# Regrouping the gate/up block products of a hybrid encoder layer: four weight sums a side, three chained pairs, plain token order

## The chip, the cores and the metric

The kernel runs on one core of a Trainium2 chip. A core has a matmul engine (PE, with its weight loads shown apart as PEld), a vector engine (DVE), a scalar engine (ACT), a third elementwise engine (POOL) and SP, whose queue issues most DMAs. Each works off its own instruction queue in order, and they meet at semaphores. Elementwise operands lie in on-chip memory (SBUF); matmul results lie in banks of PSUM, which ACT and DVE read out ("evacuate"). The metric is device microseconds of one launch, the median of several runs.

## The reference, cut to what matters

```python
def encoder_layer(x, ...):
    h = rmsnorm(x, attn_norm_g)
    proj = h @ w_in
    ...
    mix = jnp.concatenate([rmsnorm(a, mla_out_g), rmsnorm(b, na_out_g)], axis=-1)
    x = x + mix @ w_o
    h2 = rmsnorm(x, ffn_norm_g)
    x = x + (jax.nn.silu(h2 @ w_gate) * (h2 @ w_up)) @ w_down
    return x
```

Two sequences (256 and 1024 tokens, model width 1024, FFN width 2816) go through the layer in float32 and then through a last norm. The change touches `h2 @ w_gate` and `h2 @ w_up`, and what prepares `h2`.

## The kernel before, in words

The 1280 tokens are ten tiles of 128. Every float32 operand of a matmul is split into two fp32r parts, hi (a cast, on ACT) and lo (the rest, a subtraction on DVE or POOL), and `mm3` (L108) issues three matmuls: hi by hi, hi by lo, lo by hi.

**Stages.** Projections and attention come first. The output projection follows (691 to 830 us of the profile): for each token tile t, `mix_in` prepares the mixed heads, `out_proj` runs 48 matmuls of 512 columns into `po` and adds the residual (L786), and `ffn_in` (L788) makes the normalised `h2` (Square on ACT L792, its root on POOL L89/L91, the scaling on DVE L795), transposes it into two PSUM banks of 4 x 128 columns (L818) and reads those out, times a gain, into the four activation blocks R11, R12, R21, R22 (first digit: upper or lower half of the model width; second: tokens 0 to 639 or 640 to 1279; held in tiles zA and zB). Then gate and up run together, and then the down projection (matmuls into `d`).

**Gate and up.** The product of a weight panel (2 x 2 blocks A of 512 x 128) and the activations (2 x 2 blocks R) is made with seven block products instead of eight (Strassen's way). There are 11 panels `fp` and two sides (gate i=0, up i=1). Product m multiplies a weight operand `wc` (a block or a sum of blocks, split into hi and lo) by an activation operand `S[m]` (a block or a sum of blocks, split likewise): 4 slices kc x 3 matmuls x 2 halves s of 320 columns, so 24 matmuls into two banks `M`. In all 11 x 2 x 7 x 24 = 3696 matmuls.

`operand` (L862) makes a weight operand: the sum on POOL (L870, five of the seven products have one), the cast on ACT (L873), the lo on POOL (L874); three operands fit in `wc`. `S[1]` and `S[3]` are built tile by tile in the output projection; the others (6, 5, 2, 4, 7) in the first panel, by `build_S`: a sum on DVE or POOL (L838), a cast on ACT (L843) and a lo on DVE (L844). `product` reads a finished bank once or twice: a copy on ACT (L931), or an add or subtraction on DVE (L934, L936). `finish` makes the silu (ACT L949), gate times up (DVE L951), and the sums and stores of the activations for the down projection (L964, L70).

**Order.** Token tiles go 0, 5, 1, 6, 2, 7, 3, 8, 9, 4, so that the sums of R blocks of two token halves can be made early. Products go 3, 6, 1, 5, 2, 4, 7; in the first panel 3 and 1 first, mixed over sides and halves. The order on PE, ACT, DVE and POOL is fixed when the program is built, by a scheduler that keeps program order only where it is told (`tc.issue_after`); on the chip each engine follows its list.

Of the kernel before, what the change touches and what calls it, by code (L numbers as in the profile page):

```python
# [11 lines left out]
F32 = mybir.dt.float32  # L12
# [27 lines left out]
def encoder_trunk(ctx: ExitStack, tc: tile.TileContext, x_tm, x_T, g_attn, w_c, w_v, w_qk,  # L40
# [67 lines left out]
    def mm3(out, sh, sl, mh, ml, first, last):  # L108
        nc.tensor.matmul(out, lhsT=sh, rhs=mh, start=first, stop=False)  # L109
        nc.tensor.matmul(out, lhsT=sh, rhs=ml, start=False, stop=False)  # L110
        nc.tensor.matmul(out, lhsT=sl, rhs=mh, start=False, stop=last)  # L111
# [605 lines left out]
    for x in reversed(lstack):  # L717
# [14 lines left out]
         3: [rC.tile([P, 4, NQ], F32R, name="S3", bufs=2) for x in "hl"]}  # L732
# [55 lines left out]
    def ffn_in(t, x, sum1=None):  # L788
# [9 lines left out]

        def evacuate(eng, q, tr, add=None):
            for i in range(4):  # L800
                s = gf[:, 4 * q + i:4 * q + i + 1]
                o = R[f"{q + 1}{t // 5 + 1}"][:, i, c0:c0 + P]
                if add is not None:
                    eng.scalar_tensor_tensor(out=sum1[:, i], in0=tr[:, i], scalar=s,
                                             in1=add[:, i, c0:c0 + P], op0=ALU.mult, op1=ALU.add)
                elif eng is nc.scalar:
                    eng.activation(o, tr[:, i], AF.Copy, scale=s)
                else:
                    eng.tensor_scalar(out=o, in0=tr[:, i], scalar1=s, scalar2=1.0,
                                      op0=ALU.mult, op1=ALU.mult)  # L810

        tr = []
        for q in range(2):
            tr.append(po.tile([P, 4, P], F32, name="trm" if t in order[-2:] and q else "trh",
                              bufs=1))
            for i in range(4):
                kc = 4 * q + i
                nc.tensor.transpose(tr[q][:, i], h2[:, kc * P:(kc + 1) * P], ident)  # L818
            if sum1 is None:
                evacuate(nc.vector if q else nc.scalar, q, tr[q])  # L820
            elif q == 0:
                evacuate(nc.vector, 0, tr[0], R["22"])
        if sum1 is not None:
            out = split_S(1, slice(c0, c0 + P), sum1)
            with tc.issue_after(out[0]):
                evacuate(nc.scalar, 0, tr[0])
            evacuate(nc.vector, 1, tr[1])
            return out


    B_OP = {1: ("11", ALU.add, "22"), 3: ("12", ALU.subtract, "22"), 6: ("11", ALU.add, "12"),
            5: ("22",), 2: ("11",), 4: ("21", ALU.subtract, "11"), 7: ("21", ALU.add, "22")}

    SUM = {6: R["12"], 4: R["11"], 7: R["21"], 5: R["22"], 2: R["11"]}

    def sum_S(m, cs, eng, out=None):
        a, op, b = B_OP[m]
        return eng.tensor_tensor(out=SUM[m][:, :, cs] if out is None else out,  # L838
                                 in0=R[a][:, :, cs], in1=R[b][:, :, cs], op=op).ins

    def split_S(m, cs, src=None):
        src = SUM[m][:, :, cs] if src is None else src
        i0 = nc.scalar.copy(out=S[m][0][:, :, cs], in_=src)  # L843
        i1 = nc.vector.tensor_sub(out=S[m][1][:, :, cs], in0=src, in1=S[m][0][:, :, cs])  # L844
        return i0.ins, i1.ins

    def make_S(m, cs, eng):
        tmp = rY.tile([P, 4, P], F32, name="sum", bufs=2)
        sum_S(m, cs, eng, tmp)
        return split_S(m, cs, tmp)  # L850

    A_OP = {1: ("11", ALU.add, "22"), 3: ("11",), 6: ("21", ALU.subtract, "11"),
            5: ("11", ALU.add, "12"), 2: ("21", ALU.add, "22"), 4: ("22",),
            7: ("12", ALU.subtract, "22")}

    def load_A(src, fp, blocks, at=None):
        A = {}
        for b in blocks:
            nm = at[b] if at else b
            A[b] = rY.tile([P, 4, P], F32, name=f"A{nm}", bufs=2 if nm == "11" else 1)  # L860
            load(A[b], src[fp, int(b[0]) - 1, int(b[1]) - 1])
        return A  # L862

    def operand(A, m):
        if len(A_OP[m]) == 1:
            raw = A[A_OP[m][0]]
        else:
            a, op, b = A_OP[m]
            raw = rY.tile([P, 4, P], F32, name="sum", bufs=2)
            nc.gpsimd.tensor_tensor(out=raw, in0=A[a], in1=A[b], op=op)  # L870
# [5 lines left out]

    src = (w_gate, w_up)

    def first(m, i):
        at = {"11": "11", "12": "21", "21": "12", "22": "11"} if i else None  # L880
        return operand(load_A(src[i], 0, [b for b in A_OP[m] if isinstance(b, str)], at), m)

    pm = [pool("pm0", space=PSUM, side="right")]
    order = (0, 5, 1, 6, 2, 7, 3, 8, 9, 4)
    cur = mix_in(order[0])
    w31 = {}
    for n, t in enumerate(order):
        with tc.issue_after(last_split[0]):
            nxt = mix_in(order[n + 1]) if n + 1 < NT else None
        if n == 6:  # L890
            w31 = {(m, i): first(m, i) for m, i in ((3, 0), (3, 1), (1, 0))}
        out_proj(t, *cur)
        cs = slice((t % 5) * P, (t % 5 + 1) * P)
# [372 lines left out]
```

## Time and profile before

| | us |
|---|---|
| median of 3 runs | 1672.1 (1670.27 to 1674.97) |
| the profiled execution, its own time | 1669.73 |
| its span, first to last instruction | 1667.8 |
| PE busy (PEld, DVE, ACT, POOL) | 1607.0 (1450.4, 950.5, 751.4, 689.2) |

```profile
PE   7999999999899999999989999999999998999998
DVE  4653044445677777544486555444555546855776
ACT  5534154444577777544354333333333333333434
POOL 3451434353011119234387666767666650000102
```

The four rows are from the page's picture of the span in 40 slices of 41.7 us, a digit being the busy share in tenths. The output projection lies in slices 17 to 20, gate and up in 20 to 33, the down projection behind. PE is close to full in nearly all; the eight in slice 21 is the passage from the output projection to gate and up, that in slice 34 the passage to the down projection. POOL is busiest in gate and up, where it makes the weight sums and the lo parts, and still has three to four tenths free.

### The profile page before, as it was taken

How to read it: one execution, taken by the hardware profiler on the slowest of the kernel's cores; microseconds unless marked ns; L12 is line 12 of the kernel's file. 1: busy time of each engine (PE TensorE's matmuls, PEld its weight loads, DVE VectorE, ACT ScalarE, POOL GpSimd, SP SyncE). 2: the span in 40 equal slices, each digit the busy share in tenths (PEclk: the TensorE clock that was granted, in tenths of full speed). 3: DMA queues.
4: the chain of work that ended last, by engine and by line, in shares of the span. 5: the costliest groups of instructions: out<-in, count | busy, mean ns of one | idle time of the engine just before them, and what ended most of it. 6: DMA issues, size and time to landing. Idle time of an engine off the chain costs nothing.

```text
span 1667.8 us, 26037 instructions
## 1 busy us (share of the span) xinstructions
PE 1607.0 (96%) x9601; PEld 1450.4 (87%) x9601; DVE 950.5 (57%) x1641; ACT 751.4 (45%) x1565; POOL 689.2 (41%) x818
## 2 busy tenths in 40 slices
PE   7999999999899999999989999999999998999998
PEld 7987899987688888888879999999999997788886
DVE  4653044445677777544486555444555546855776
ACT  5534154444577777544354333333333333333434
POOL 3451434353011119234387666767666650000102
PEclk9999999999999999999999999999999999999999
DMA  6635302134001013234332322222322219733434
GB/s 225 207 108 141 67 23 61 36 114 145 20 19 34 20 29 99 76 122 144 115 108 94 107 93 86 76 90 83 107 106 81 77 64 358 245 93 95 147 104 150
DMA packets 125231, 173.75 MB, mean 104 GB/s; under 512 B 35568, under 2 KB 67184, under 8 KB 125104
## 3 DMA queue, kind: packets, MB, share of 16 engines
q1 hardware_dynamic: 80864, 122.92, 23.3%
q10 hardware_dynamic: 43680, 46.87, 8.2%
q0 software_dynamic: 560, 2.29, 0.3%
q8 instruction: 76, 1.25, 0.3%
q14 instruction: 51, 0.42, 0.1%
HBM read 121.58 MB, written 50.46 MB: 103 GB/s over the span
## 4 chain that ended last, share of the span: by engine, by line
PE 84%; issue 4%; DMA 4%; POOL 3%; ACT 2%; DVE 2%; SPq 0%; POOLq 0%; ACTq 0%; DVEq 0%
PE M L111 10%; PE M L110 10%; PE M L109 10%; PE d L110 5%; PE d L109 5%; PE d L111 5%; PE o L685 3%; PE tp L678 3%; PE na_o L461 2%; PE po L109 2%; PE pj L109 2%; PE pj L111 2%; PE pj L110 2%; PE po L110 2%; PE po L111 2%
## 5 line engine op out<-in xcount | busy, mean ns | idle before, releaser
L109 PE MATMUL M<-S,wc 128*128 128x320 f32 x1056 | 326.8, 310 | 2.8 <-ACT wc L873 2.3
L110 PE MATMUL M<-S,wc 128*128 128x320 f32 x1056 | 327.4, 310 | 2.1 <-DVE S L844 2.0
L111 PE MATMUL M<-S,wc 128*128 128x320 f32 x1056 | 325.3, 310 | 1.4 <-POOL wc L874 1.4
L109 PEld LDWEIGHTS M<-S,wc 128*128 128x128 f32 x1056 | 198.9, 188 | 3.8 <-ACT wc L873 2.8
L110 PEld LDWEIGHTS M<-S,wc 128*128 128x128 f32 x1056 | 198.8, 188 | 3.2 <-DVE S L844 3.1
L874 POOL TENSOR_TENSOR wc<-sum,wc 128x512 fp32r<-128x512 f32 x110 | 148.7, 1353 | 128.0 <-ACT wc L873 125.7
L111 PEld LDWEIGHTS M<-S,wc 128*128 128x128 f32 x1056 | 198.2, 188 | 1.9 <-POOL wc L874 1.9
L870 POOL TENSOR_TENSOR sum<-A,A 128x512 f32<-128x512 f32 x110 | 162.3, 1483 | 13.6 <-DMA A<-in_w_gate_dram 4.2
L873 ACT CAST wc<-sum 128x512 fp32r<-128x512 f32 x110 | 68.0, 622 | 188.2 <-PE M L110 142.8
L110 PE MATMUL d<-w,ah 128*128 128x512 f32 x385 | 147.4, 398 | 2.5 <-DVE w L1029 2.5
L109 PE MATMUL d<-w,ah 128*128 128x512 f32 x385 | 144.5, 400 | 4.2 <-ACT ah L1028 4.2
L111 PE MATMUL d<-w,ah 128*128 128x512 f32 x385 | 145.4, 398 | 0.4 <-DVE ah L1029 0.4
L934 DVE TENSOR_TENSOR z<-M,z 128x320 f32<-128x320 f32 x144 | 67.8, 485 | 88.0 <-PE M L111 51.1
L100 DVE TENSOR_TENSOR PT<-tp,PT 128x512 fp32r<-128x512 f32 (+1 forms) x144 | 93.1, 658 | 40.6 <-ACT PT L99 39.2
L1028 ACT CAST ah<-as 128x640 fp32r<-128x640 f32 x77 | 56.0, 727 | 121.7 <-issue 71.3
L934 DVE TENSOR_TENSOR zB<-M,zB 128x320 f32<-128x320 f32 x120 | 56.6, 486 | 81.2 <-PE M L111 47.6
L99 ACT CAST PT<-tp 128x512 fp32r<-128x512 f32 (+1 forms) x144 | 79.1, 564 | 42.4 <-PE tp L678 39.3
L109 PEld LDWEIGHTS d<-w,ah 128*128 128x128 f32 x385 | 73.1, 190 | 22.8 <-ACT ah L1028 5.0
L1029 DVE TENSOR_TENSOR ah<-as,ah 128x640 fp32r<-128x640 f32 x77 | 64.1, 836 | 50.4 <-ACT ah L1028 50.4
L670 DVE TENSOR_REDUCE mm<-S 128x1 f32<-128x1024 f32 (+1 forms) x80 | 84.8, 1061 | 12.7 <-PE S L111 11.2
L698 POOL TENSOR_TENSOR ob<-ob 128x128 f32<-128x128 f32 x40 | 18.4, 461 | 177.5 <-ACT ob L695 177.3
L110 PEld LDWEIGHTS d<-w,ah 128*128 128x128 f32 x385 | 72.7, 189 | 20.7 <-DVE w L1029 3.2
(384 smaller groups left out, 4004.8 us busy)
## 6 DMA issues: line engine op xcount, KB each, us to landing
as<-act_d SPq DMA_DIRECT2D x77, 320.0 KB
A<-in_w_gate_dram SPq DMA_DIRECT2D x52, 256.0 KB
A<-in_w_up_dram SPq DMA_DIRECT2D x52, 256.0 KB
act_d<-z ACTq DMA_DIRECT2D x35, 320.0 KB
act_d<-zB ACTq DMA_DIRECT2D x35, 320.0 KB
x<-in_x_tm_dram SPq DMA_DIRECT2D x20, 512.0 KB
cT_d<-stg ACTq DMA_DIRECT2D x20, 320.0 KB
w<-in_w_down_dram SPq DMA_DIRECT2D x11, 512.0 KB
```

The costliest lines, as they stand in the source:

```text
L99: i = nc.scalar.copy(out=hi, in_=ps)
L100: nc.vector.tensor_sub(out=lo, in0=ps, in1=hi)
L109: nc.tensor.matmul(out, lhsT=sh, rhs=mh, start=first, stop=False)
L110: nc.tensor.matmul(out, lhsT=sh, rhs=ml, start=False, stop=False)
L111: nc.tensor.matmul(out, lhsT=sl, rhs=mh, start=False, stop=last)
L670: nc.vector.reduce_max(out=nm[:, u:u + 1], in_=S, axis=AX.X, negate=True)
L870: nc.gpsimd.tensor_tensor(out=raw, in0=A[a], in1=A[b], op=op)
L873: i0 = nc.scalar.copy(out=hi, in_=raw)
L874: i1 = nc.gpsimd.tensor_tensor(out=lo, in0=raw, in1=hi, op=ALU.subtract)
L934: nc.vector.tensor_add(out=o, in0=ps, in1=o)
L1028: nc.scalar.copy(out=o[:, 0], in_=raw)
L1029: nc.vector.tensor_sub(out=o[:, 1], in0=raw, in1=o[:, 0])
```

## The change

The seven products are grouped in another way (still seven, still 3696 matmuls). With s1 = A21 + A22, s2 = s1 - A11, s4 = A12 - s2 and A21' = A11 - A21 a side needs four sums; products 1 and 2 take plain blocks A11 and A12. On the activation side R11 and R21 are used plainly by products 1 and 2, and for tokens 640 to 1279 the blocks are combined as they leave PSUM. Second members of the pairs 1-2, 7-4 and 5-3 go on accumulating in the PSUM bank of the first (`CHAIN`, `held`, `onto`), after that bank has been read once; so a bank is read once for each of the seven products. The order of products is 1, 2, 6, 7, 4, 5, 3, that of tokens 0 to 9.

For tokens 0 to 639, `ffn_in` splits R11 and R21 straight into S1 and S2. For tokens 640 to 1279 both banks of a tile are read twice, slice by slice: ACT writes the plain block, and DVE (`scalar_tensor_tensor`) writes R12 - R11 or R22 - R21 over the old block. Then come a further sum T2 into a tile of its own and R21 - T2 (POOL; DVE for the last tile). S6 is cast from T2 by token tiles.

In the first panel four products (1 and 2, of gate and of up) come first, the operands of three of them made at token tile 6; the six other weight blocks of the panel are loaded, once the output projection has ended, into memory that will later hold S5 (`spare`), and the sums of both sides are made there before product 6.

```diff
-    A_OP = {1: ("11", ALU.add, "22"), 3: ("11",), 6: ("21", ALU.subtract, "11"),
-            5: ("11", ALU.add, "12"), 2: ("21", ALU.add, "22"), 4: ("22",),
-            7: ("12", ALU.subtract, "22")}
...
+            for i in range(4):
+                s = gf[:, 4 * q + i:4 * q + i + 1]
+                o = R[f"{q + 1}{t // 5 + 1}"][:, i, cs]
+                if t < 5 and q:
+                    nc.vector.tensor_scalar(out=o, in0=tr[q][:, i], scalar1=s, scalar2=1.0,
+                                            op0=ALU.mult, op1=ALU.mult)
+                else:
+                    nc.scalar.activation(o, tr[q][:, i], AF.Copy, scale=s)
+                if t >= 5:
+
+                    d = R["12" if q else "11"][:, i, cs]
+                    nc.vector.scalar_tensor_tensor(out=d, in0=tr[q][:, i], scalar=s, in1=d,
+                                                   op0=ALU.mult, op1=ALU.subtract)
+        if t < 5:
+            split_S(1, cs)
+            split_S(2, cs)
+            return
+        eng = nc.vector if t == NT - 1 else nc.gpsimd
...
+        eng.tensor_tensor(out=T2[t - 5], in0=R["22"][:, :, cs], in1=R["11"][:, :, cs],
+                          op=ALU.subtract)
+        return eng.tensor_tensor(out=R["21"][:, :, cs], in0=R["21"][:, :, cs], in1=T2[t - 5],
+                                 op=ALU.subtract).ins
...
+    def operand(A, m, s2=None, s4=None):
+        if m == 6:
...
+            sum_A(A["s1"], A["21"], A["22"], ALU.add)
+            sum_A(A["s2"], A["s1"], A["11"])
+            w = split_A(A["s2"])
...
+            sum_A(A["s4"], A["12"], A["s2"])
+            return w
+        if m == 7:
+            sum_A(A["21"], A["11"], A["21"])
+        return split_A(A[{1: "11", 2: "12", 7: "21", 4: "22", 5: "s1", 3: "s4"}[m]])
...
-    order = (0, 5, 1, 6, 2, 7, 3, 8, 9, 4)
...
-    SEQ2 = (3, 6, 1, 5, 2, 4, 7)
+    SEQ = (1, 2, 6, 7, 4, 5, 3)
+    CHAIN = {2: 1, 4: 7, 3: 5}
...
+        if m not in CHAIN:
+            held[s] = pm[bank].tile([P, 512], F32, name=f"M{bank}", bufs=4)[:, 0:NS]
+        ps = held[s]
...
             mm3(ps, w[0][:, kc], w[1][:, kc], S[m][0][:, kc, cs], S[m][1][:, kc, cs],
-                kc == 0, kc == 3)
...
+                kc == 0 and m not in CHAIN, kc == 3, m in CHAIN)
...
+            for n, (b, i) in enumerate((("12", 1), ("21", 0), ("22", 0), ("21", 1), ("22", 1),
+                                        ("12", 0))):
+                A0[i][b] = load_A(i, 0, b, at[n])
+            for i in range(2):
+                for m in (1, 2):
+                    for s in range(2):
+                        product(C[i], w0[m, i], m, s, held[i], 0)
+                    finish(G, U, i, m, fp)
+                if i == 0:
+                    w0[2, 1] = operand(A0[1], 2)
+            for n, m in enumerate(SEQ[2:]):
+                w = [operand(A0[i], m, at[6 + i], ("A21", "A22")[i]) for i in range(2)]
+                if m != 3:
+                    build_S(SEQ[n + 3], w[1][2:])
```

Three places show what the scheduler made of it. The first is ACT's list at the last token tile. Before, `zA<-trh` of x4 reads one whole bank (half of the last tile), `M0` and `M1` are product banks, and `wc` operands:

```order
L843 CAST S1_7998<-sum_9192 128x4x128
L807 ACTIVATE zA_8002<-trh_9201,gf_8022 128x128 x4
L843 CAST S6_9243<-zA_8003 128x4x320
L931 COPY z_9250<-M0_9341 128x320
L843 CAST S6_9243<-zA_8003 128x4x320
L931 COPY z_9249<-M1_9326 128x320
L873 CAST wc_9377<-sum_9375 128x512
L931 COPY z_9250<-M1_9356 128x320
L873 CAST wc_9387<-sum_9385 128x512
```

In the changed kernel `trh_9121` and `trm_9134` are the banks of token tile 8, `trh_9210` and `trm_9223` those of tile 9, `M0_9278` and `M0_9292` hold product 2 of gate, `wc_9333` is the operand of product 2 of up:

```order
L813 ACTIVATE zA_8003<-trh_9121,gf_8022 128x128
L914 COPY z_9268<-M0_9292 128x320
L931 ACT_TABLE_LOAD
L931 ACTIVATE z_9268<-z_9268 128x640
L813 ACTIVATE zB_8005<-trm_9134,gf_8022 128x128
L813 ACTIVATE zA_8003<-trh_9121,gf_8022 128x128
L813 ACTIVATE zB_8005<-trm_9134,gf_8022 128x128
L813 ACTIVATE zA_8003<-trh_9210,gf_8022 128x128
L838 CAST S6_9256<-sum_9147 128x4x128
```

The one piece of four reads has become sixteen single reads a tile (eight on ACT), and among those of tile 8 now stand the copies of product 2 and the first silu with its table load. ACT's list goes on, to the last reads of tile 9 and what stands behind them:

```order
L813 ACTIVATE zA_8003<-trh_9210,gf_8022 128x128
L813 ACTIVATE zB_8005<-trm_9223,gf_8022 128x128
L813 ACTIVATE zA_8003<-trh_9210,gf_8022 128x128
L813 ACTIVATE zB_8005<-trm_9223,gf_8022 128x128 x2
L838 CAST S6_9256<-A12_9236 128x4x128
L845 CAST wc_9333<-S5_9270 128x512
L914 COPY z_9269<-M0_9337 128x320
```

The cast of up's operand stands behind the last read of tile 9 and an S6 cast.

The second place is POOL's list behind the last token tile, to the first lo of a product with sums. Before, `sum` and `wc` alternate in pairs, gate and up:

```order
L838 TENSOR_TENSOR zA_8003<-zA_8002,zA_8003 128x4x128
L870 TENSOR_TENSOR sum_9375<-A21_9371,A11_9373 128x512
L870 TENSOR_TENSOR sum_9385<-A12_9381,A11_9383 128x512
L874 TENSOR_TENSOR wc_9378<-sum_9375,wc_9377 128x512
L874 TENSOR_TENSOR wc_9388<-sum_9385,wc_9387 128x512
L870 TENSOR_TENSOR sum_9457<-A11_9453,A12_9455 128x512
L870 TENSOR_TENSOR sum_9467<-A11_9463,A21_9465 128x512
```

Changed, `wc_9334` is the lo of product 2 of up, `sum_9392` and `sum_9401` are s1 of gate and of up, and `wc_9396` is the lo of product 6 of gate:

```order
L846 TENSOR_TENSOR wc_9334<-S5_9270,wc_9333 128x512
L856 TENSOR_TENSOR sum_9392<-S5_9270 128x512
L856 TENSOR_TENSOR sum_9401<-S5_9270 128x512
L856 TENSOR_TENSOR S5_9271<-sum_9392,A11_8807 128x512
L856 TENSOR_TENSOR S5_9270<-A11_8807,S5_9270 128x512
L856 TENSOR_TENSOR S5_9271<-sum_9401,A11_8819 128x512
L856 TENSOR_TENSOR S5_9270<-A11_8819,S5_9270 128x512
L856 TENSOR_TENSOR A21_9399<-S5_9271 128x512
L846 TENSOR_TENSOR wc_9396<-S5_9271,wc_9395 128x512
```

Where two sums stood ahead of a lo, seven now stand between the two lo parts; s2 of both sides, both A21' and gate's s4 lie there.

The third place is PE's list in the changed kernel where product 2 of up (`M_9337`, `M_9351`) ends and product 6 (`S_9256`) and 7 (`S_9410`) begin; L110 is hi by hi, L111 hi by lo (of the activations), L112 lo (of the weights) by hi:

```order
L112 MATMUL M_9351<-S_8000,wc 128x320
L110 MATMUL M_9416<-S_9256,wc 128x320
L111 MATMUL M_9416<-S_9257,wc 128x320
L110 MATMUL M_9430<-S_9256,wc 128x320
L111 MATMUL M_9430<-S_9257,wc 128x320
L110 MATMUL M_9444<-S_9256,wc 128x320
L111 MATMUL M_9444<-S_9257,wc 128x320
L110 MATMUL M_9458<-S_9256,wc 128x320
L111 MATMUL M_9458<-S_9257,wc 128x320
L110 MATMUL M_9488<-S_9410,wc 128x320
L111 MATMUL M_9488<-S_9411,wc 128x320
L110 MATMUL M_9502<-S_9410,wc 128x320
L112 MATMUL M_9416<-S_9256,wc 128x320
```

Eleven matmuls that need only the cast part of their weight operand have been put ahead of the first L112 of product 6, which needs the lo part.

## Prediction on record

> **What bounds the kernel now.** I began with the page's first part: an engine busy nearly all the span can only be helped by taking work off it.
>
> ```profile
> PE 1607.0 (96%) x9601; PEld 1450.4 (87%) x9601; DVE 950.5 (57%) x1641; ACT 751.4 (45%) x1565; POOL 689.2 (41%) x818
> ```
>
> The change leaves PE's 3696 product matmuls as they are. Next I asked for busy time by stretches: first the product matmuls (M) alone, then all work. A row has the stretch in us, its length, each engine's busy time with instructions, the granted clock, the DMA share and GB/s.
>
> ```profile
> 690.00:829.60 139.60, 6.23 (x36) 5.54 (x37) 0.00 (x0) 0.18 (x1) 1.00 0.34 115
> 829.60:895.00 65.40, 56.47 (x356) 53.77 (x357) 14.24 (x32) 7.51 (x20) 0.97 0.31 105
> 895.00:1379.00 484.00, 484.00 (x3304) 484.00 (x3303) 148.21 (x319) 62.47 (x156) 1.00 0.25 89
> ...
> 700.00:829.00 129.00, 128.94 (x640) 105.43 (x639) 56.17 (x95) 47.73 (x116) 47.88 (x65) 1.00 0.37 123
> 840.00:845.00 5.00, 3.25 (x19) 2.50 (x17) 4.53 (x5) 2.56 (x5) 5.00 (x3) 1.00 0.15 52
> 845.00:850.00 5.00, 4.44 (x21) 4.44 (x22) 2.66 (x3) 2.97 (x4) 4.56 (x4) 0.66 0.47 157
> 870.00:875.00 5.00, 3.31 (x23) 3.05 (x22) 5.00 (x8) 3.07 (x5) 5.00 (x3) 1.00 0.44 122
> ```
>
> From 895 to 1379 us nothing is lost: 484.00 / 3304 = 0.1465 us a matmul. The output projection is full too (128.94 of 129). The passage between loses: 356 x 0.1465 = 52.2, and 0.85 for the last tile's eight transposes, of 65.4, so **12.4 us are lost in 829.6 to 895**. The timeline says at what:
>
> ```profile
> 830.16 0.68 DVE L786 TENSOR_TENSOR x<-po,x 128x512 f32<-128x512 f32 x1
> 831.00 1.10 ACT L792 ACTIVATE m<-x 128x1024 f32<-128x1024 f32 x1
> 832.56 0.56 POOL L91 TENSOR_TENSOR rh<-rh,mhalf 128x1 f32<-128x1 f32 x1
> 833.15 1.78 DVE L795 TENSOR_SCALAR m<-x,rh 128x1024 f32<-128x1024 f32 x1 [1.48 <-POOL rh L91]
> 834.99 0.66 PE L818 MATMUL trh<-ident,m 128*128 128x128 f32 x4 [0.76 <-DVE m L795]
> 837.37 1.14 ACT L807 ACTIVATE zA<-trh,gf 128x128 f32<-128x128 f32 x4
> 839.84 5.01 POOL L870 TENSOR_TENSOR sum<-A,A 128x512 f32<-128x512 f32 x2
> 843.08 0.41 PE L109 MATMUL M<-S,wc 128*128 128x320 f32 x1 [0.94 <-ACT wc L873]
> 844.82 2.50 POOL L874 TENSOR_TENSOR wc<-sum,wc 128x512 fp32r<-128x512 f32 x2
> 845.56 0.63 PE L109 MATMUL M<-S,wc 128*128 128x320 f32 x1 [1.36 <-ACT wc L873]
> 846.26 0.47 PE L109 MATMUL M<-S,wc 128*128 128x320 f32 x1
> 846.52 0.47 PE L110 MATMUL M<-S,wc 128*128 128x320 f32 x1
> ```
>
> PE waits for the last tile's chain (add, Square, root, scaling), then for weight operands whose sums take POOL 2.5 us each, and runs some 11 matmuls 0.26 apart at the 0.66 clock (1.3 us more than at 0.1465).
>
> The other loss is at the far end: the last M starts at 1379.23, the down projection at 1381.99.
>
> ```profile
> 1379.23 0.31 PE L111 MATMUL M<-zA,wc 128*128 128x320 f32 x1
> 1381.99 0.50 PE L109 MATMUL d<-w,ah 128*128 128x512 f32 x1 [2.46 <-ACT ah L1028]
> 1382.33 0.39 PE L110 MATMUL d<-w,ah 128*128 128x512 f32 x1
> 1383.74 0.39 PE L110 MATMUL d<-w,ah 128*128 128x512 f32 x1
> 1388.79 0.33 SPq L64 DMA_DIRECT2D x<-xm_d  x1
> 1393.38 0.69 DVE L1065 TENSOR_TENSOR ws<-w 128x512 f32<-128x512 f32 x1 [4.32 <-DMA w<-in_w_down_dram]
> ...
> 1379.40:1395.40 16.00, 11.27 (x45) 8.17 (x45) 0.00 (x0) 0.00 (x0) 1.00 0.90 330
> ```
>
> 45 d matmuls at (1383.74 - 1382.33) / 6 = 0.235 are 10.5 us of 16, so **5.5 us lost**. SP's list stands at `x<-xm_d` until the last activation stores are out (1388.79), and the weight behind it arrives for 1393.38. Beyond these 18 us the change has nothing to win.
>
> **The change part by part.**
>
> *Sums and reads that go.* 22 weight sums leave POOL, 132 adds leave DVE (an output half is added to five times, not eight), 88 copies leave ACT.
>
> ```profile
> L870 POOL TENSOR_TENSOR sum<-A,A 128x512 f32<-128x512 f32 x110 | 162.3, 1483 | 13.6 <-DMA A<-in_w_gate_dram 4.2
> L934 DVE TENSOR_TENSOR z<-M,z 128x320 f32<-128x320 f32 x144 | 67.8, 485 | 88.0 <-PE M L111 51.1
> L931 ACT COPY z<-M 128x320 f32<-128x320 f32 x80 | 32.0, 426 | 43.3 <-PE M L111 20.5 <-DMA act_d<-zB 13.6 <-DVE zB L964 8.7
> ```
>
> That is 22 x 1.48 = 33 us of POOL, 132 x 0.485 = 64 of DVE, 88 x 0.426 = 37 of ACT, all but a few beside the full PE of 895 to 1379. Value: 0.
>
> *Evacuation in the output projection.* Tiles 5 to 9 have 16 alternate reads where ACT and DVE had four each beside one another; T2 and R21 on POOL take the place of like sums. A tile has 12.9 us (129 / 10) and ACT is busy 4.8 of them (47.73 / 10). Eight rounds of ACT 0.37 and DVE 0.34 are 5.7; with hand-offs 6.3. PE's 48 `po` matmuls of the next tile cover it: 0, except for tile 9, which has no next tile.
>
> *The passage.* Let T0 be the end of the last `po` matmul. In the new PE list 48 M stand ahead of it, not 36. Durations:
>
> ```profile
> L795 DVE TENSOR_SCALAR m<-x,rh x10: 744/749/1779, 710.6 to 833.2; 128x1024 f32<-128x1024 f32 x10
> L807 ACT ACTIVATE zA<-trh,gf 128x128 f32<-128x128 f32 x36 | 10.3, 368 | 32.1 <-PE trh L818 32.1
> L809 DVE TENSOR_SCALAR zB<-trh,gf 128x128 f32<-128x128 f32 x32 | 8.9, 342 | 0.0
> L838 DVE TENSOR_TENSOR sum<-zA,zB x5: 683/693/1379, 735.2 to 828.2; 128x512 f32<-128x512 f32 x5
> L949 ACT ACT_TABLE_LOAD  x1: 1283/1283/1283, 862.5 to 862.5; - x1
> L949 ACT ACTIVATE z<-z x24: 739/740/742, 863.8 to 1355.5; 128x640 f32<-128x640 f32 x24
> L873 ACT CAST wc<-sum 128x512 fp32r<-128x512 f32 x12 | 7.5, 622 | 15.3 <-POOL sum L870 11.1 <-PE M L110 4.2
> L870 POOL TENSOR_TENSOR sum<-A,A x110: 1282/1296/2568, 792.3 to 1360.5; 128x512 f32<-128x512 f32 x110
> L870 POOL TENSOR_TENSOR sum<-A,A 128x512 f32<-128x512 f32 x12 | 24.2, 2027 | 2.9 <-DMA A<-in_w_gate_dram 2.5 <-PE M L110 0.3
> L874 POOL TENSOR_TENSOR wc<-sum,wc 128x512 fp32r<-128x512 f32 x12 | 20.0, 1677 | 3.9 <-ACT wc L873 3.9
> ```
>
> 1. After T0 PE has 24 M (product 2 of gate) and four waiting transposes of tile 8: till T0+4.0. Tile 9's scaled rows are ready at about T0+4.2 (before: T0+5.3, of which 1.0 was the one slow L795).
> 2. Their transposes need a bank that tile 8's reads still hold. ACT's list has, ahead of these, the copy of product 2 (0.43, waiting for PE), the table load (1.28) and the silu (0.74); two reads and hand-offs are 1.2. So T0+4.0+3.7 = 7.7: **3.7 idle**. Transposes to 8.6.
> 3. Sixteen alternate reads with an S6 cast between, 4.4, T2 on DVE 0.69, the last S6 cast 0.62, and only then, in ACT's list, the cast of up's product 2 (0.62): T0+15.0, **6.4 idle**. Before, two reads of 1.1 us and one cast stood there.
> 4. That operand's lo (POOL, 1.3) comes at 16.4: **1.4 idle**; then product 2 of up runs till T0+20.
> 5. POOL, waiting since T0+4 behind that lo, has seven sums and product 6's lo to do: 8 operations. At the least time, 1.282, they end at 26.7; at this passage's means (2.03 and 1.68) at 32.3; the median 1.296 and the mean 1.483 lie near the low end. I take 1.6, since DVE has half as much to do there as before: 29.2. PE has 11 ready matmuls meanwhile (1.6): **7.6 idle**.
> 6. One spell of low clock, as before: 1.3; that after the first two pieces lies ahead of another wait.
>
> Sum: 3.7 + 6.4 + 1.4 + 7.6 + 1.3 = 20.4, against 12.4: **+8**. With the low POOL price 17.9, and 16.5 if the reads go faster by 1.4 (no hand-offs seen): +4. With the high one 23.5, with a second spell of clock 24.8: +12. Behind product 6 every operand of the panel is summed already, and PE needs 48 M (7.0 us) a pair of operands: 0 more.
>
> The Trainium skill, "SBUF — State Buffer", section "Who interferes with whom", says that a DVE instruction with two SBUF inputs and a GpSimd instruction that reads SBUF exclude each other for a whole instruction. The trace agrees (L870: 1282 at the least, 2568 at the most). An estimate by that page: some 4 us of such DVE work (the S6 and S7 lo parts) lie beside step 5, so the eight operations would end at 30.7 and the sum would be +9.5.
>
> The Trainium skill, "TensorE: Matmul & The Clock Gate", section "HAM oscillation — how this bites in real kernels", has an idle window of about 3.4 us halve the clock for the time after. The row 845:850 (0.66) agrees; were each of the three long pieces charged the page's half of 3.4 us, an estimate of 5.1 would replace 1.3.
>
> *Chained pairs, steady panels.* The second product of a pair must wait until the bank of the first is read: 0.43 or 0.49 after its last matmul. No row of before has such a wait. PE's new list puts 14 to 24 other M between (2.0 to 3.5 us), which covers it; cover gone, three pairs by 21 sides at 0.5 would be 31. ACT's reads stand behind silus (0.74) and stores, so I expect a few misses: **+1**, from 0 to 6.
>
> *The far end.* Gate and up's last S7 is read 72 M before the end, where S2 was read 48 before, so the first loads of the down projection, which need its room, start 24 x 0.1465 = 3.5 us sooner; the last stores are issued about 0.9 sooner. **-2**, from 0 to -3.5: next late is the weight behind `x<-xm_d`, which the stores still hold.
>
> Sum: +8 + 1 - 2 = +7 on the profiled execution's 1669.7 (span 1667.8 and 1.9 around it): 1676.7. That execution lies 2.4 below the median of 1672.1, so for the median 1679.
>
> **Rivals.** A measurement of this kernel can tell about 0.3% (5 us) from no change: 1667 to 1677 is "the same".
>
> *A: POOL is free and quick.* If the sums run at 1.29 as in most of the trace and the reads overlap better, the passage costs +4, with no steady loss and -3 at the end: 1673. For it: the median of L870. Against: the means of L870 and L874 in this passage. It covers also the case that the change does what it says (fewer sums and reads) and the time hardly moves because PE was the bound.
>
> *B: chained pairs stall in every side.* If an ACT read behind a silu and a store comes 0.6 us late at one pair of each of 21 sides, 21 x 0.6 = 12.6 come on top: 1691. For it: slack of some pairs is below 0.5 us by my count. Against: ACT is busy under half of 895 to 1379.
>
> *C: faster.* All sums of the panel are made under the last tile, and product 6 never waits. PE has 59 M and 8 transposes (9.5 us) between T0 and the first need of product 6's lo; the passage gains 5 us from the point where that lo is ready by T0+15.6 (9.5, 12.4 - 5 = 7.4 lost, less 1.3 of clock). The price would be -5 and -2 at the end: 1665. For it: POOL is idle from T0+4 to T0+15 and blocks arrive in time. Against: the lists, which hold POOL at the lo of step 4 until then.
>
> **How the numbers follow.** Forecast (1677 to 1688) 0.48, A 0.32, B 0.10, C 0.10. Faster 0.10, same 0.32, slower 0.58. Time 1679; the range 1669 to 1688 leaves out B and C. Its low end is A with the whole 5.5 of the far end (1672.1 + 4 - 5.5 = 1670.6), and 1.8 less, as far as the runs of before lie below their median; its high end is the passage at +12 and half of the chains' 6 with 1 gained at the end, 1686, and 2 for the runs' spread.
>
> **What would show it.** In the changed profile: PE idle of about 4 us ahead of tile 9's transposes, with the silu's table load on ACT in it; of about 6 ahead of product 2 of up, ended by its cast; of about 8 ahead of product 6's lo by hi, ended by POOL; 100% PE in the windows from 900 to 1370; the gap after the last M near 0.5 to 3. The prediction is wrong if the passage loses under 14 us, if the steady windows show PE below 99%, or if POOL's sums there take 1.3.

## The result and the profile after

The changed kernel takes 1681.62 us (median of 4 runs, 1678.56 to 1682.94), beside 1671.37 for the kernel before: a ratio of 1.0055, 95% interval [1.0034, 1.0076]. A second series gave 1681.01 and 1.0055 [1.0037, 1.0074]. It is slower by about half a per cent, 10 us; the forecast was slower too, by 7 us: 1679, with a range from 1669 to 1688. Of the launches in the table of the experiments one, of the kernel with the late silu, took 5058.28 us and is left out of its median.

The page of the changed kernel: its row of PE's busy time, and PE and the granted clock in 40 slices.

```profile
PE 1612.6 (96%) x9601; PEld 1455.7 (87%) x9601; DVE 888.3 (53%) x1521; ACT 724.6 (43%) x1500; POOL 645.3 (38%) x795
PE   7999999999899999999969999999999999999998
PEclk9999999999999999999979999999999999999999
```

DVE has 62 us less to do, POOL 44 and ACT 27, where the prediction had counted 64, 33 and 37. PE has the same 9601 instructions, and in slice 21, the passage from the output projection to gate and up, PE falls from eight tenths to six and its clock to seven. The same place by stretches (the first three rows product matmuls alone, the others all work, with POOL's column):

```profile
900.00:1300.00 400.00, 399.87 (x2728) 399.61 (x2728) 77.76 (x164) 27.40 (x65) 1.00 0.27 90
836.00:843.50 7.50, 3.76 (x24) 3.52 (x24) 0.00 (x0) 1.01 (x3) 1.00 0.79 281
843.50:870.00 26.50, 14.46 (x51) 12.70 (x52) 0.49 (x1) 0.85 (x2) 0.56 0.10 32
...
843.50:846.00 2.50, 1.90 (x8) 1.49 (x8) 0.85 (x3) 1.46 (x5) 2.30 (x2) 0.50 0.00 0
858.40:865.70 7.30, 3.51 (x11) 2.41 (x11) 4.02 (x3) 3.74 (x5) 7.30 (x6) 0.65 0.36 117
865.70:870.00 4.30, 4.24 (x16) 4.24 (x17) 1.85 (x2) 0.00 (x0) 4.30 (x4) 0.50 0.00 0
870.00:895.00 25.00, 25.00 (x170) 25.00 (x169) 17.52 (x23) 12.86 (x16) 11.78 (x8) 0.98 0.08 26
```

The panels behind it are full (399.87 of 400). From 836 (T0, the end of the last `po`, is 835.9) to 895 PE starts 243 product matmuls (24 + 51 + 170, less the two that run across 870 and stand in both rows) and ten transposes (eight of tile 9, two still of tile 8), 36.7 us of work in 59: **22.3 us are lost where 12.4 were**. The timeline says at what:

```profile
840.47 1.28 ACT L931 ACT_TABLE_LOAD   x1
841.77 0.74 ACT L931 ACTIVATE z<-z 128x640 f32<-128x640 f32 x1
842.79 0.35 DVE L817 SCALAR_TENSOR_TENSOR zA<-trm,gf,zA 128x128 f32<-128x128 f32 x1 [2.60 <-ACT zB L813]
843.46 1.09 PE L805 MATMUL trh<-ident,m 128*128 128x128 f32 x4 [3.46 <-DVE zA L817]
850.64 0.63 PE L110 MATMUL M<-S,wc 128*128 128x320 f32 x1 [5.25 <-ACT wc L845]
850.67 1.81 POOL L846 TENSOR_TENSOR wc<-S,wc 128x512 fp32r<-128x512 f32 x1 [4.43 <-ACT wc L845]
852.53 0.63 PE L112 MATMUL M<-S,wc 128*128 128x320 f32 x1 [0.45 <-POOL wc L846]
853.10 3.34 POOL L856 TENSOR_TENSOR sum<-S 128x512 f32<-128x512 f32 x2 [0.63 <-DVE S L839]
861.46 0.63 PE L110 MATMUL M<-S,wc 128*128 128x320 f32 x1 [2.20 <-ACT wc L845]
865.76 0.63 PE L112 MATMUL M<-S,wc 128*128 128x320 f32 x1 [0.23 <-POOL wc L846]
866.20 0.47 PE L110 MATMUL M<-S,wc 128*128 128x320 f32 x1
866.46 0.47 PE L111 MATMUL M<-S,wc 128*128 128x320 f32 x1
```

PE waits for tile 9's transposes while ACT loads the silu's table and DVE waits for ACT's next read; then for the cast of up's product 2, and POOL has waited 4.43 for the same cast. From its lo on, POOL works without a pause worth the name to product 6's lo (865.7), and PE gets casts one at a time. The matmuls between are 0.26 apart.

The other end of gate and up:

```profile
1384.27 0.38 SPq L64 DMA_DIRECT2D w<-in_w_down_dram  x1
1394.48 0.31 PE L112 MATMUL M<-zA,wc 128*128 128x320 f32 x1
1395.06 0.48 DVE L916 TENSOR_TENSOR z<-M,z 128x320 f32<-128x320 f32 x1
1395.46 0.68 DVE L1055 TENSOR_TENSOR ws<-w 128x512 f32<-128x512 f32 x1
1396.17 0.62 ACT L1015 CAST w<-ws 128x512 fp32r<-128x512 f32 x1 [11.37 <-DVE ws L1055]
1397.47 0.51 PE L110 MATMUL d<-w,ah 128*128 128x512 f32 x1 [2.68 <-ACT ah L1015]
1402.84 0.33 SPq L64 DMA_DIRECT2D x<-xm_d  x1
...
1394.65:1410.65 16.00, 12.19 (x50) 9.26 (x51) 0.00 (x0) 0.00 (x0) 1.00 0.69 250
```

The first weight is asked for 10.2 us before the last M (1394.48 - 1384.27), before 6.7, so 3.5 sooner as worked out. Yet the first `d` comes 3.0 behind the last M (before 2.8): DVE's `ws`, which it needs, stands in DVE's list behind the last sums of gate and up and starts with no idle time ahead of it; ACT's casts of the weight and of `ah` follow. It was so in the profile of before:

```profile
1379.57 0.49 DVE L934 TENSOR_TENSOR z<-M,z 128x320 f32<-128x320 f32 x1 [0.54 <-PE M L111]
1379.98 0.68 DVE L1065 TENSOR_TENSOR ws<-w 128x512 f32<-128x512 f32 x1
```

The last row above is the `d` matmuls alone in 16 us from just behind the last M, as the prediction's row of before was cut. It has 50 where that one had 45, but the second profiles of the two kernels have it the other way round: 50 before (1377.56 to 1393.56), 45 changed (1392.96 to 1408.96). And `x<-xm_d` comes 8.4 us behind the last M in both profiles of the changed kernel, 9.6 and 8.4 in those of before.

**Where the 12.7 us between the two profiled executions (1682.38 and 1669.73) come from.** I cut each profile at three matmuls, the first and the last `po` and the last M, whose starts the views of the tiles `po` and `M` give; for the changed kernel:

```profile
L110 PE MATMUL po<-wo,mT x160: 389/394/504, 700.4 to 835.2; 128*128 128x512 f32 x160
L112 PE MATMUL po<-wo,mT x160: 392/394/483, 701.8 to 835.6; 128*128 128x512 f32 x160
L112 PE MATMUL M<-zA,wc x176: 305/309/309, 895.0 to 1394.5; 128*128 128x320 f32 x176
```

| us | first po at | to last po | to last M | first po to last M | to the end |
|---|---|---|---|---|---|
| before | 695.2 | 134.3 | 549.7 | 684.0 | 288.6 |
| before, second profile | 693.1 | 134.2 | 550.1 | 684.3 | 285.9 |
| changed | 700.4 | 135.2 | 558.9 | 694.1 | 286.1 |
| changed, second profile | 698.8 | 135.3 | 558.7 | 694.0 | 287.3 |

The middle is steady to 0.3 us, and the change costs **9.9 us there**. The two outer parts spread by several us from one profile to the next.

### The profile page after: what moved, and what is told of

Same layout as the page of the kernel before. It is cut to its first block, busy times and chain, and to the rows that moved or that the text cites. A ratio compares the mean times of both kernels' runs of the same rounds, so it can differ in the third digit from the quotient of the medians.

```text
span 1680.6 us, 25657 instructions
## 1 busy us (share of the span) xinstructions
PE 1612.6 (96%) x9601; PEld 1455.7 (87%) x9601; DVE 888.3 (53%) x1521; ACT 724.6 (43%) x1500; POOL 645.3 (38%) x795
## 4 chain that ended last, share of the span: by engine, by line
PE 83%; issue 4%; DMA 3%; POOL 3%; DVE 3%; ACT 2%; SPq 0%; ACTq 0%; POOLq 0%; DVEq 0%
PE M L112 10%; PE M L110 10%; PE M L111 10%; PE d L111 5%; PE d L110 5%; PE d L112 5%; PE o L686 3%; PE tp L679 3%; PE po L110 2%; PE pj L110 2%; PE po L112 2%; PE po L111 2%; PE pj L111 2%; PE pj L112 2%; PE na_o L462 2%
## 5 line engine op out<-in xcount | busy, mean ns | idle before, releaser
L110 PE MATMUL M<-S,wc 128*128 128x320 f32 x1056 | 324.7, 312 | 9.6 <-ACT wc L845 9.5
L111 PE MATMUL M<-S,wc 128*128 128x320 f32 x1056 | 326.7, 311 | 0.0
L112 PE MATMUL M<-S,wc 128*128 128x320 f32 x1056 | 314.0, 311 | 0.7 <-POOL wc L846 0.7
L110 PEld LDWEIGHTS M<-S,wc 128*128 128x128 f32 x1056 | 199.8, 190 | 11.4 <-ACT wc L845 11.2
L111 PEld LDWEIGHTS M<-S,wc 128*128 128x128 f32 x1056 | 200.3, 190 | 0.3
L112 PEld LDWEIGHTS M<-S,wc 128*128 128x128 f32 x1056 | 196.5, 189 | 1.6 <-POOL wc L846 1.5
L846 POOL TENSOR_TENSOR wc<-A,wc 128x512 fp32r<-128x512 f32 x85 | 119.0, 1402 | 85.6 <-ACT wc L845 84.0
L111 PE MATMUL d<-w,ah 128*128 128x512 f32 x385 | 145.8, 397 | 2.5 <-DVE w L1016 2.5
L110 PE MATMUL d<-w,ah 128*128 128x512 f32 x385 | 143.4, 397 | 3.7 <-ACT ah L1015 3.7
L112 PE MATMUL d<-w,ah 128*128 128x512 f32 x385 | 143.7, 396 | 0.0
L916 DVE TENSOR_TENSOR z<-M,z 128x320 f32<-128x320 f32 x120 | 57.0, 488 | 141.7 <-PE M L112 131.3
L845 ACT CAST wc<-A 128x512 fp32r<-128x512 f32 x85 | 52.8, 622 | 167.2 <-PE M L111 145.9
L846 POOL TENSOR_TENSOR wc<-sum,wc 128x512 fp32r<-128x512 f32 x62 | 87.8, 1415 | 86.4 <-ACT wc L845 86.4
L916 DVE TENSOR_TENSOR zB<-M,zB 128x320 f32<-128x320 f32 x100 | 47.6, 488 | 133.3 <-PE M L112 126.7
L845 ACT CAST wc<-sum 128x512 fp32r<-128x512 f32 x62 | 38.4, 619 | 149.8 <-PE M L111 104.1
L110 PEld LDWEIGHTS d<-w,ah 128*128 128x128 f32 x385 | 72.4, 188 | 22.2 <-ACT ah L1015 4.8
L111 PEld LDWEIGHTS d<-w,ah 128*128 128x128 f32 x385 | 72.5, 188 | 20.5 <-DVE w L1016 2.9
```

Source lines behind the costliest of these rows:

```text
L845: i0 = nc.scalar.copy(out=hi, in_=raw)
L846: i1 = nc.gpsimd.tensor_tensor(out=lo, in0=raw, in1=hi, op=ALU.subtract)
L916: nc.vector.tensor_add(out=o, in0=ps, in1=a)
```

## The experiments

What each gave, with the stretch from the first po to the last M beside the time:

| | median us (runs) | ratio to before, 95% | first po to last M |
|---|---|---|---|
| changed again | 1681.01 (6) | 1.0055 [1.0037, 1.0074] | 694.0 |
| POOL's sums in another order | 1680.77 (6) | 1.0049 [1.0030, 1.0069] | 695.7 |
| silu late | 1677.75 (11) | 1.0038 [1.0023, 1.0053] | 691.5 |
| product 1 behind the output projection | 1680.63 (6) | 1.0054 [1.0035, 1.0074] | 695.3 |
| sums early | 1672.26 (12) | 1.0014 [1.0002, 1.0025] | 685.3 |
| sums early, silu late | 1670.98 (12) | 0.9999 [0.9987, 1.0012] | 683.0 |
| the same, tile 8's T2 on DVE, cast ahead | 1671.53 (12) | 1.0007 [0.9993, 1.0020] | 685.8 |
| before again | 1665.28 (1) | - | 684.3 |
| sums early, silu late, cast ahead | 1668.35 (12) | 0.9988 [0.9976, 0.9999] | 683.9 |
| reads from SBUF | 1678.18 (5) | 1.0041 [1.0025, 1.0056] | 690.3 |
| sums, silu, cast, reads | 1669.14 (11) | 0.9990 [0.9977, 1.0003] | 681.1 |
| the same, two lists reordered | 1669.12 (12) | 0.9990 [0.9975, 1.0004] | 680.9 |

The series were taken at different times, each beside launches of the kernel of before, so times of different series are best compared by their ratios. The times follow the stretch to within a few us; what tells the kernels apart is the stretch and the waits in it.

**The two kernels again.** No edit.

> The changed kernel once more, unaltered. Of the 12.7 us between the two profiled executions 5.1 lie ahead of the output projection (its first po matmul at 700.4 us, before 695.2), where both programs have the same list of instructions. Theory A (the executions differ there by chance): this profile's first po matmul lies anywhere from 695 to 701, and the median is 1679 to 1682. Theory B (the changed program is slower there each time): again 700 to 701, and the median 1681 to 1683. Both: the passage from the last po to the last M matmul again takes 558 to 560 us (before: 549.7).

> The kernel of before once more, for a second profile: the stretch from the last po to the last M matmul 549 to 551 us as in the first, with 12.4 us lost behind the output projection; its first po matmul anywhere from 695 to 701 if the spread ahead of the output projection is chance.

Theory A fits better. Of the 5.1 us ahead of the output projection, where both programs have the same lists, the second pair of profiles shows 5.7 again, but profiles of changed kernels whose lists differ only later lie between 695.1 and 701.5, and the medians (a difference of 9 to 10) leave no room for 5 us beside the 9.9. Both stretches came again (558.7, 550.1).

**POOL's sums in another order.** Each side's s1 and s2, then its lo; the other sums behind both.

```diff
-                w = [operand(A0[i], m, at[6 + i], ("A21", "A22")[i]) for i in range(2)]
+                if m == 6:
+                    w = [operand(A0[0], 6, at[6], "A21", True)]
+                    with tc.issue_after(w[0][3]):
+                        w.append(operand(A0[1], 6, at[7], "A22", True))
```

(`True` leaves the s4 sum to the next product; products behind 6 stand behind `w[1][3]`, up's lo.)

> Only POOL's list is altered: product 6 of gate gets s1, s2 and its lo first, then up's s1, s2 and lo, and only then the two A21' and s4 sums. Theory (the seven sums ahead of product 6's first lo are 8 us of the passage): that lo ends some 13.3 us after the lo of up's product 2 less five operations, so 7 to 8 us sooner than in the changed kernel (865.7 - T0 of 835.9 = 29.8 there, here 22 to 23); up's product 6 follows with three operations per 3.5 us of PE; 5 to 7 us faster than the changed kernel. Rival (another wait takes over: S7's lo parts on DVE, up's operand): PE loses at product 7 what it won at product 6, 0 to 2 us faster.

```profile
854.53 0.41 PE L112 MATMUL M<-S,wc 128*128 128x320 f32 x1 [0.50 <-POOL wc L846]
865.43 0.41 PE L110 MATMUL M<-S,wc 128*128 128x320 f32 x1 [1.39 <-ACT wc L845]
869.72 0.63 PE L112 MATMUL M<-S,wc 128*128 128x320 f32 x1 [3.44 <-POOL wc L846]
...
859.67 5.05 POOL L856 TENSOR_TENSOR S<-A,S 128x512 f32<-128x512 f32 x2
```

These are PE's waits and a POOL row of that kernel's timeline (T0 is 831.9 here). Product 6's lo comes at T0+22.6, 7 us sooner, as expected; but product 7 then waits 1.39 and 3.44 for its own operand, behind four other sums on POOL, two of which take 5.05. The stretch is 1.5 to 1.7 longer. The rival holds: this other order of POOL's list gains nothing; what costs would then be how much POOL has still to do when it may begin, which the early sums below test.

**The first silu later.**

```diff
-                    finish(G, U, i, m, fp)
+                    if (m, i) != (2, 0):
+                        finish(G, U, i, m, fp)
                 if i == 0:
                     w0[2, 1] = operand(A0[1], 2)
+                    with tc.issue_after(w0[2, 1][2]):
+                        finish(G, U, 0, 2, fp)
```

> Only the first silu (with its table load) is put behind the cast of up's product 2 on ACT. Theory (the silu holds the banks of token tile 8): tile 9's transposes start 2.0 us sooner (T0+5.6, not T0+7.6) and all that follows with them; 2 us faster than the changed kernel. Rival (the alternate reads of tile 8 on two engines hold the banks as long as before, or POOL's list, not the transposes, sets the end): under 0.7 us faster.

```profile
836.19 0.66 PE L805 MATMUL trh<-ident,m 128*128 128x128 f32 x4 [1.43 <-DVE zA L817]
842.59 0.64 PE L110 MATMUL M<-S,wc 128*128 128x320 f32 x1 [5.22 <-ACT wc L845]
857.72 0.63 PE L112 MATMUL M<-S,wc 128*128 128x320 f32 x1 [2.86 <-POOL wc L846]
```

The wait ahead of the transposes goes from 3.46 to 1.43, and the stretch is 2.5 shorter, the time 3.3. So the silu and its table load did hold tile 8's banks; the next wait (5.22) is untouched.

**Product 1 kept for behind the output projection.** Products 1 and 2 inside `with tc.issue_after(last_po):`, the last `po` matmul.

> Only PE's list is altered: the 48 matmuls of product 1, which the changed kernel does between the matmuls of the output projection, where PE is full anyway, now stand behind its last po matmul. The same work in all. Theory (PE's waits behind the output projection are empty because the ready products were used up before): PE has 72 matmuls (10.6 us) in place of 24 there; T0 comes 7 us sooner, the wait of 3.5 us ahead of tile 9's transposes goes, the others stay; 3 to 5 us faster than the changed kernel. Rival (tile 8's transposes, which now stand behind 27 of these matmuls, delay tile 9's, and POOL's list ends as much later): within 1 us of it.

Behind the last po it came as expected: 561.3 with 48 more matmuls in it (7.0 us), so 554.3 against 558.9, and the wait ahead of tile 9's transposes is gone. But the 480 po matmuls now take 134.0, where 135.2 had held the 48 as well: 5.8 us more than the 128.2 they should take. PE's longest wait there, and the clock behind it (two more waits are of 0.68 and 0.57):

```profile
788.54 0.76 PE L806 MATMUL trh<-ident,m 128*128 128x128 f32 x4 [2.16 <-DVE zA L818]
...
780.00:790.00 10.00, 7.84 (x39) 6.17 (x38) 3.10 (x7) 4.98 (x11) 5.99 (x7) 0.95 0.36 131
790.00:800.00 10.00, 10.00 (x42) 8.11 (x41) 2.85 (x6) 3.46 (x11) 4.90 (x8) 0.88 0.48 158
```

The premise that PE was full there anyway is false: it was full because of these matmuls. They hid the alternate reads of earlier tiles (DVE zA, L818 here). The time came within 1 us of the changed kernel, as the rival had it, but for this reason.

**POOL's sums while tile 9 is read.** T2 of tiles 5 and 6 go where s1 will be, S6's lo parts need no longer follow tile 9, and s1 and s2 of both sides come before up's product 2.

```diff
-        nm = ("A21", "A22", "sum", "sum", "A12")[t - 5]
+        nm = ("sum", "sum", "A21", "A22", "A12")[t - 5]
...
-    build_S(6, (last,))
+    build_S(6, ())
...
+                sum_A(A0[i]["s1"], A0[i]["21"], A0[i]["22"], ALU.add)
+                early = sum_A(A0[i]["s2"], A0[i]["s1"], A0[i]["11"])
...
+                    with tc.issue_after(early):
+                        w0[2, 1] = operand(A0[1], 2)
```

> The stretch from the start of the last po matmul to that of the last M matmul is 558.9 and 558.7 us in the two profiles of the changed kernel, 549.7 in that of before, 560.4 with POOL's list in another order. Here POOL makes s1 and s2 of both sides ahead of the lo of up's product 2, in the time in which it waits for that operand's cast (T0+4 to T0+15); for that the S6 lo parts on DVE no longer stand behind tile 9, and s1 takes the room of T2 of tiles 5 and 6. Theory (POOL has as much to do as the passage is long, and starts too late): product 6's first lo at T0+18.6, not 29.8; the stretch 549 to 551, the time 8 to 10 us below the changed kernel, near that of before. Rival (a later wait takes it back, as with the other order of POOL's list: product 7's operands or S7): the stretch 555 or more.

POOL's rows and PE's waits (T0 is 834.7):

```profile
845.04 1.72 POOL L856 TENSOR_TENSOR sum<-S 128x512 f32<-128x512 f32 x1
851.11 5.79 POOL L846 TENSOR_TENSOR wc<-S,wc 128x512 fp32r<-128x512 f32 x3
...
851.09 0.64 PE L110 MATMUL M<-S,wc 128*128 128x320 f32 x1 [6.82 <-ACT wc L845]
```

Four sums run from 845.0 to 851.0, where POOL had stood idle, and the three lo parts end at 856.9, product 6's among them. Behind the 6.82 PE has no wait of note. From the first po to the last M it is 685.3, 8.7 us less (550.0 behind the last po, where 549 to 551 was expected); the ratio falls from 1.0055 to 1.0014, some 7 us. This names the cause of most of the loss: **not the sums, but that they began 17 us behind the last po** (853.1). One thing was not tested apart: with the edit three of S6's five lo parts on DVE also come before tile 9 (835.5 to 837.4), where in the changed kernel all five come behind it (850.1 to 855.3). The early sums need this for their memory, and it frees DVE in the passage.

**Both.** `finish` of product 2 moved behind the casts of product 6, on top.

> As the kernel with the early sums, and the first silu with its table load behind the casts of product 6. Theory (the gains add, since the transposes of tile 9 and POOL's sums then both come sooner): the stretch 2 us shorter again, 547 to 549, the time 1669 to 1672. Rival (POOL's four sums behind tile 8's T2 set the lo of up's product 2, not the transposes): under 0.7 us shorter than without.

The stretch behind the last po is 547.7, 2.3 shorter, as expected; the time is level with that of the kernel before (0.9999).

**Tile 8's T2 on DVE, the cast ahead; and the cast alone.** `eng = nc.vector if t >= NT - 2 else nc.gpsimd`, and `build_S(6, ())` placed behind `w0[2, 1]` with its last part behind that cast.

> As that kernel, with T2 and R21 of tile 8 on DVE, so that POOL's sums start at T0+3, and with the cast of up's product 2 ahead of the last S6 cast on ACT. Theory: that cast 1.3 us sooner, its lo at T0+12.5; the stretch 545 to 547, the time 1667 to 1670, below the kernel of before. Rival (PE now waits for S6's last lo part on DVE, which the two casts and DVE's further sums delay): no shorter than with the late silu alone.

> The kernel with the early sums and the late silu, and the cast of up's product 2 ahead of the last S6 cast on ACT; T2 of tile 8 stays on POOL. The kernel that also gave tile 8's T2 and R21 to DVE missed: its stretch from the last po to the last M was 550.5, not 545 to 547, and without both edits 547.7. Theory (DVE's two sums stood among the alternate reads of tile 9): without them the cast's move shows, 546.4 to 547.2. Rival (the move of the cast itself costs, since the last S6 parts then come later and PE has them ahead of product 2's rest): 548 or more.

Both missed: 550.5 and 548.6 behind the last po. From the first, DVE's list and PE's wait:

```profile
841.12 1.76 DVE L826 TENSOR_TENSOR A<-zB,zA 128x512 f32<-128x512 f32 x1
844.68 1.75 DVE L839 TENSOR_TENSOR S<-A,S 128x512 fp32r<-128x512 f32 x1
...
853.08 0.64 PE L111 MATMUL M<-S,wc 128*128 128x320 f32 x1 [1.03 <-DVE S L839]
```

Two sums (the first is shown) and a lo, 0.68 each on DVE alone, take 1.7 beside POOL's sums and stand among the reads of tile 9. Without them, in the second kernel, product 2 starts 2 us sooner than without the cast ahead, but S6's last lo comes later and PE has product 6's first matmuls ahead of product 2's rest: it waits there (1.05). The rivals hold in both.

**Reads from SBUF.** The only edit to the changed kernel:

```diff
-                if t >= 5:
-                    d = R["12" if q else "11"][:, i, cs]
-                    nc.vector.scalar_tensor_tensor(out=d, in0=tr[q][:, i], scalar=s, in1=d,
-                                                   op0=ALU.mult, op1=ALU.subtract)
+            if t >= 5:
+                d = R["12" if q else "11"][:, :, cs]
+                nc.vector.tensor_tensor(out=d, in0=R[f"{q + 1}2"][:, :, cs], in1=d,
+                                        op=ALU.subtract)
```

> The changed kernel with one edit: for tokens 640 to 1279 ACT alone reads the transposed banks, and DVE then subtracts from the copy in SBUF, one 128x512 instruction a bank in place of four reads of PSUM. From the first po to the last M matmul it is 694.1 and 694.0 us in the changed kernel, 684.0 and 684.3 in that of before. Theory (the alternate reads hold the banks): the wait ahead of tile 9's transposes (3.46) goes, the cast of up's product 2 comes 3 to 4 us sooner and POOL's list with it; 689.5 to 691. Rival (DVE's subtractions, with both inputs in SBUF, and POOL's sums hold each other up): 692.5 or more.

690.3, within the theory's 689.5 to 691, and no wait is left ahead of tile 9's transposes; the cast of up's product 2 comes at T0+11.9, not T0+14.7. The alternate reads were worth some 4 us of the loss, part of it the same wait that the late silu shortens.

**All together, and the two lists.** Sums early, silu late, the cast ahead and reads from SBUF; then also product 6 behind product 2 on PE (`tc.issue_after(mm2)`), and POOL's list as s1 of gate, product 2's lo, and each further lo as soon as its sum is there.

> All that paid, together: early sums, late silu, the cast ahead, and the reads from SBUF. Theory (the three add, as they shorten different waits): product 2 of up starts at T0+9 to 10, POOL's sums are done by T0+10.5; first po to last M 677 to 680 us, the time 1663 to 1667, below before (684.1; 1670.7). Rival (S6's last lo part on DVE, ahead of which PE does not get to the rest of product 2, or POOL and DVE holding each other up): 682 or more.

> The kernel with all that paid came to 681.1 us from the first po to the last M, not 677 to 680: PE had matmuls of product 6 ahead of the rest of up's product 2 and waited for product 6's casts (2.84) and S6's last lo (1.04), and POOL made all four sums ahead of product 2's lo. Here product 6 stands behind product 2 on PE, and POOL makes s1 of gate, then that lo, then the other sums, each lo as soon as its sum is there. Theory (the order of the two lists is what is left): no wait above 1.5 us behind the cast of product 2; 679 to 680 us, the time 1667 to 1669, 2 to 4 us below before. Rival (POOL, at 1.6 to 1.75 us an operation beside DVE, is the bound again in any order): 681 or more.

681.1 and 680.9: both miss the theory, the second by one us, though its waits are small; in the first, POOL's first sum also waited 2.78 for a weight block to arrive (`DMA S<-in_w_gate_dram`). From the second:

```profile
843.53 0.42 PE L110 MATMUL M<-S,wc 128*128 128x320 f32 x1 [2.34 <-ACT wc L844]
867.73 0.43 PE L112 MATMUL M<-S,wc 128*128 128x320 f32 x1 [1.34 <-POOL wc L845]
...
861.42 2.54 POOL L855 TENSOR_TENSOR A<-S 128x512 f32<-128x512 f32 x1
```

What seems to be left is POOL at up to 2.5 us an operation, and the chain to the cast; no run takes these away. In the profile these kernels are 3 us shorter than that of before; in time, 0.9990 with intervals that reach 1.0003 and 1.0004, they cannot be told from it. The one interval that lies below 1, 0.9988 [0.9976, 0.9999], belongs to a kernel whose stretch is as long as before, so I claim no gain from it.

## Why the prediction was right

Step by step, the profile of the changed kernel (T0 = 835.9) beside the forecast:

| step | forecast | measured |
|---|---|---|
| sums and reads that go | 0 | 0: PE busy 399.87 of 400 us |
| output projection | 0 | -0.8: 135.2 with 12 more M (1.76) against 134.3 |
| 2, transposes of tile 9 | T0+7.7, 3.7 idle | T0+7.6, 3.46 |
| 3, cast of up's product 2 | T0+15.0, 6.4 idle | T0+14.7, 5.25 |
| 4, its lo | T0+16.4, 1.4 idle | T0+16.6, 0.45 |
| 5, product 6's lo | T0+29.2, 7.6 idle | T0+29.9, 4.4 |
| 6, low clock behind it | 1.3 | 2.4 |
| half pace between the waits | in the idle time | 6.3 |
| the passage | 20.4 lost, +8 | 22.3 lost, +9.9 |
| chained pairs | +1 | 0 |
| the far end | -2 | 0 |

- The chain of times held to 0.7 us at each step; that the silu, the alternate reads and POOL's late start make it is shown by taking each away (2.5, some 4, and 8.7 us of the stretch, which overlap).
- Within steps 3 to 5 less was idle than forecast, because transposes and matmuls between ran at half pace: the twenty of product 2 from 852.53 on took 5.1 us, not 2.9, and PE still waited 0.60 for the next cast. The idle pieces are 13.6 (3.46 + 5.25 + 0.45 + 4.44), so 8.7 of the 22.3 are slow work, and 6.3 of these lie ahead of another wait. Step 6 was under-sized: 19 matmuls from 865.76 to 870.93 took 5.17, 2.4 more than at 0.1465. The prediction's estimate by the Trainium skill ("TensorE: Matmul & The Clock Gate", "HAM oscillation — how this bites in real kernels") of a loss after each of the three pieces, 5.1, is too much, and one such spell, 1.7, too little. That an idle window of about 3.4 us halves the clock agrees with the row at 843.5 (0.50, behind 3.46 idle); but the prediction's own row 845:850 (0.66) lay behind pieces of at most 1.36, so it does not bear that out as the prediction says.
- Step 5's price of 1.6 an operation held: eight from 852.5 to 865.7, 1.65 each. But the one wait of about 8 us ended by POOL did not come as such: PE waited 0.60, 2.20 and 1.41 for casts, the first two of them made as soon as POOL had the sum, the third behind two S7 casts on ACT, and 0.23 for the lo itself.
- **Chained pairs**: nothing is lost to them in the panels. The one pause from 900 to 1300 is of 0.3 us ahead of a matmul at 1004.0, and ends as the cast of a weight operand does (1003.96), not with a read of a bank. The covering matmuls suffice, and rival B falls.
- **The far end** is the step that failed. The loads did start 3.5 us sooner, but the step took the first load for what ends last. DVE's `ws` behind the last sums does (the first `d` comes 3.0 behind the last M, 2.8 before), and the wait for `x<-xm_d` is no shorter than in the second profile of before. The ends do not differ beyond their spread: 288.6 and 285.9 before, 286.1 and 287.3 changed. So 0 was measured where -2 was forecast.
- Rival A, that POOL is quick and the passage costs +4, falls with the 1.65. Rival C's mechanism (sums made under the last tile) is right as a mechanism: built, it gives back 8.7 us of the stretch. It was not what the lists did. POOL was idle from T0+4 to T0+15, as rival C had it, but for tile 8's two sums (843.6 to 846.2).

Passage, chains and end sum to +9.9 + 0 + 0; of the forecast's +7 the passage was 2 short, the chains 1 too dear and the end 2 too hopeful. The table's -0.8 of the output projection would bring the parts to +9.1, where the stretch from the first po to the last M shows +9.9; what makes up the rest stays open.

## What to carry to other kernels

Where the bound engine was full, in the steady state, fewer operations on the others were worth nothing; what the regrouping was worth was decided in the passage in front of it, by when each chain may begin. Read the new lists for what a waiting instruction holds behind it: here a lo that waited for a cast kept POOL idle while seven sums stood behind it, and moving four of them ahead gave 8.7 us of the stretch back. And work that fills an engine's row to 100% is not free to move: look at what waits it covers where it stands.

## What the runs showed that I had not expected

- The two-input DVE sums of 128x512 took 0.68 us alone and up to 1.78 beside POOL's sums, and POOL's 1.27 alone and up to 2.57 beside them. The Trainium skill, "SBUF — State Buffer", "Who interferes with whom", says that they shut each other out. Giving tile 8's two sums from POOL to DVE gained nothing here (550.5 behind the last po with it, 548.6 without).
- Ahead of the output projection the same lists took between 693.1 and 701.5 us. A difference of 0.5% between two single executions of this kernel can lie there alone; cutting the profile at fixed matmuls made steps of 1 us visible that the medians did not resolve.
